# Hybrid decoder layer on one core: the heads stage traced in three runs per pair and kept in that order on TensorE, and half of the gate projection as seven products

## The chip, the cores and the metric

The kernel runs on one core of one Trainium2 chip. The metric is the device time of one execution in microseconds (us); lower is better. A run's time is the median over several executions; beside it stands one execution with a hardware profile, on which all readings of the trace rest.

## The reference

One layer over a sequence of 2048 tokens and a model width of 1024, in float32. An input projection feeds two groups of heads that read the same normalised input: 16 state-space (Mamba-2, "SSD") heads of width 64, scanned in chunks of 128 tokens, and a short gated convolution. Both outputs (together 2048 wide) go through one output projection; its result is normalised and added to the input. At the end a gate, a 1024 x 1024 projection with a sigmoid, scales a per-layer embedding that is added.

```python
h = rmsnorm(x, norm_pre)
xbc, dt_raw, z_ssd, sc_h, sc_b, sc_c, z_sc = split(h @ w_in)
xs, bm, cm = split(silu(causal_dwconv(xbc, ssd_conv_w, ssd_conv_b)))
dt = softplus(dt_raw + dt_bias)
y_ssd = ssd_chunked(xs, dt, -exp(a_log), bm, cm, d_skip)          # 16 heads of 64, chunks of 128
y_ssd = rmsnorm(y_ssd * silu(z_ssd), ssd_norm)                    # in two groups
y_sc = sc_b * causal_dwconv(sc_c * sc_h, sc_conv_w) * silu(z_sc)
mix = concatenate([y_ssd, y_sc]) @ w_out
x = x + rmsnorm(mix, norm_post)
out = x + sigmoid(x @ w_ple_gate) * (p @ w_ple_proj)
```

## The kernel before

Tokens lie along the free dimension, model columns along the 128 partitions. The 2048 tokens are two blocks of 1024 (`b`) or four groups of 512 (`tg`). Every large product is made with both operands split into two fp32r parts (the rounded value and the rest), and three of the four cross products are taken: `PASSES`, three 128x512 matmuls per 128 of the contraction. A split is a cast on ScalarE (L134 for weights, L199 for activations) and a subtraction on VectorE (L135, L200).

Weights arrive through one list, `seq`, in the order of their use. The class `Weights` keeps up to six split pieces of 128 x 4 x 128 ready (`fill`), each a load of 256 KB (L130) on SP's queue, a cast and a subtraction, and hands them out with `next`.

The program is written through a framework that tracks which instruction reads and writes which tile, sets the semaphores, and orders the instructions of each engine at compile time by its own forecast of when each is ready. The order in which the program text issues them (the order of the trace, in the words of the change) is a priority, not a command; `tc.add_manual_dep(..., NOSYNC)` fixes the order of two instructions without a semaphore. A tile pool hands a slot to a new tile when the last user of the slot's old tile is done. All loads and stores are issued on SP's queue.

The stages, one after the other, TensorE being shared between neighbours:

1. **Input projection** (to about 1032 us): products of 2x2 blocks by the seven product form (Strassen-Winograd, class `Wino`), with conv and gates behind it. Results go to DRAM: `xs_d`, `gz_d`, `cb_d`, `acs_d`, `ysc_d`, `ple_d`.
2. **Heads** (about 1032 to 1322 us). A list `steps` holds the work of the SSD heads, eight pairs of head tiles (four per block), and between the steps the generator `under()` issues `filler`: the half of the output projection that reads the short convolution (tile `os`, L838), 256 units of three matmuls, 22 of them ahead and the rest spread evenly over the steps. The work of one pair, in the names of the code and the lines of the trace:
   - `xs0`, `xs1`: load the two tiles of `xs` (L889), pool of three slots;
   - `T0`, `T1`: eight transposes each on TensorE (px, L896), then on VectorE `xd` (L903) and `xdd` (L904);
   - `load0`, `load1`: load the decays `ea` (L911, one slot, two loads of 512 KB) and the four masks `m` (L946, four slots);
   - `decays`: exp of `ea` on ScalarE (L914); `m00` to `m11`: a mask's eight exps on ScalarE (L951) and one VectorE product (L954);
   - `states`: 32 matmuls (pst, L924), then on VectorE the running state, 14 to 16 small steps (L938), and `ea` times C (L941);
   - `offsets`: 64 small matmuls from the state (py, L967);
   - `out0`, `out1`: 32 matmuls each with the masks (py, L979), then on VectorE `xs` becomes the output (L982, L983), is stored to `yz_d` (L984), squared on ScalarE (L988) and summed into `ssum` (L989).
   
   After each block `norms` adds the squares over the partitions (pn, L226) and sends the inverse norms through DRAM. `gs` makes the block's C-B products (pg, L867; pb, L879).
3. **Output projection** (to about 1512 us): `out_proj(t)` for two token groups at a time, 32 units of 24 matmuls (mo, L210); VectorE adds the part from DRAM (L1072), ScalarE squares, VectorE sums. `norm` makes the inverse norm (pn, L1084, reciprocal at L1087), `residual` scales and adds the input (L1093, L1094), `operands` splits the result.
4. **Gate** (to the end): `gate(t)`, 32 units of 24 matmuls (mg, L210); tanh on ScalarE (L1116), two VectorE steps (L1117, L1118) with the embedding `pe` (loaded at L1110), a store of 256 KB (L1119).

Steps of stages 3 and 4 are put behind numbered units (`after(unit, step)`): units 0 to 31 are the output projection, 32 to 63 the gate. Loads of two tiles at a time go through `Loads` (`L`, `L3`), three slots each.

Of the kernel before, what the change touches and what calls it, by code (L numbers as in the profile page):

```python
# [7 lines left out]
F32 = mybir.dt.float32  # L8
# [7 lines left out]
P = 128  # L16
# [38 lines left out]


@with_exitstack
def hybrid_kernel(ctx: ExitStack, tc: tile.TileContext, xT, pT, w_t, w_dt, w_o, w_g, w_p, cols_d, cst_d, outT):
# [18 lines left out]
    rs_d = [dram.tile([1, TB], F32, name=f"rs_d{b}") for b in range(NB)]  # L77
    acs_d = [dram.tile([NH, TB], F32, name=f"acs_d{b}") for b in range(NB)]

    cols = const.tile([P, NCOL], F32, name="cols")  # L80
# [56 lines left out]
    def direct(src, name, pool):  # L137
        return name, lambda sp: split_w(sp, load_w(src, name, pool), src.shape[1])
# [206 lines left out]
    for t in range(0, NG, 2):  # L345
        seq += [direct(w_o[d, :, 4 * q:4 * q + 4, :], f"o{t}_{d}_{q}", praw) for d in range(KD) for q in (0, 1)]
    for t in range(0, NG, 2):
        seq += [direct(w_g[d, :, 4 * q:4 * q + 4, :], f"g{t}_{d}_{q}", praw) for d in range(KD) for q in (0, 1)]
    W = Weights(seq)
# [3 lines left out]
    with ExitStack() as st:  # L353
# [373 lines left out]
        for b, prs, order in groups:  # L727
# [16 lines left out]
            if b + 1 < NB:  # L744
# [5 lines left out]
                if n in (6, 7, 8, 9, 10):  # L750
                    next(prep, None)

# [5 lines left out]
    class Loads:  # L758
# [5 lines left out]
        def begin(self, kind, *at):  # L764
            if (kind, *at) in self.ready:
                return
            t = self.ready[(kind, *at)] = self.pool.tile([P, 2, TG], F32, tag="ld", name="_".join(map(str, (kind, *at))))
            if kind in ("mraw", "gn"):
                b, o = divmod(at[0] * TG, TB)
            if kind == "gn":  # L770
                src = grs_d[b][:, o:o + TG].partition_broadcast(P)
            else:
                if kind == "mraw":
                    k = at[1]
                    src = yz_d[b][k:k + 2, :, o:o + TG] if k < KD else ysc_d[b][k - KD:k - KD + 2, :, o:o + TG]
                elif kind == "part":
# [37 lines left out]
    with ExitStack() as st:  # L814
# [32 lines left out]
        def heads(b):  # L847
# [34 lines left out]
            def pair(j):  # L882
# [4 lines left out]
                def loads(gr):  # L887
                    xs[gr] = t4.tile([P, TB], F32, tag="xs", name=f"xs_{b}{jts[gr]}", bufs=3)
                    nc.sync.dma_start(xs[gr], xs_d[b][jts[gr]])  # L889

                def transposes(gr):
                    jt = jts[gr]
                    px = flat(pss.tile([P, 2, TG], F32, tag="ssd", name=f"px_{b}{jt}"))
                    for c in range(NCH):
                        cs = slice(c * CH, (c + 1) * CH)
                        TE.transpose(px[:, cs], xs[gr][:, cs], ident)  # L896
                    xd[gr] = t4.tile([P, NCH, P], F32, tag="xd", name=f"xd_{b}{jt}", bufs=3)
# [113 lines left out]
        for b in range(NB):  # L1011
# [7 lines left out]
        p = pairs[0]  # L1019
        steps += [both(begins[0], p["xs0"], p["xs1"], p["load0"], p["load1"]), gs[0][0], gs[0][1], p["T0"],  # L1020
                  both(p["gz0"], p["gz1"]), p["decays"], p["T1"], no, p["m00"], no]
# [12 lines left out]
        steps += [norms[-1]]  # L1034

# [10 lines left out]


    with ExitStack() as st:
        pp = st.enter_context(tc.tile_pool(name="pp", bufs=2))
# [4 lines left out]
        def out_proj(t):  # L1054
# [25 lines left out]

        def norm(tg):

            ps = mm_bank(f"pn2_{tg}")
            TE.matmul(ps, ones_d, ssq_[tg], start=True, stop=True)  # L1084
            rs = rs_[tg] = pp.tile([P, TG], F32, tag="rs2", name=f"rs2_{tg}")
            S.activation(rs, ps, AF.Sqrt, bias=epsc[:, 0:1])
            V.reciprocal(rs, rs)  # L1087

# [11 lines left out]

        def gate(t):

            for dp in range(0, KD, 2):
                sp = []
                for tg in (t, t + 1):
                    banks = pss.tile([P, 2, TG], F32, tag="ssd", name=f"mg_{tg}_{dp}")
                    for i in range(2):
# [12 lines left out]
                        yield  # L1120


        plan = {}
# [3 lines left out]

        def second(tg, at_norm, at_res, at_ops):

            after(at_norm, lambda: norm(tg))  # L1130
# [3 lines left out]
            for n, u in enumerate(at_ops):  # L1134
                after(u, lambda d=2 * n: operands(tg, d))

        def mixes_at(tg, *units):
            m = mixes(tg, 0)
            for n, u in enumerate(units):
                after(u, *m[2 * n:2 * n + 2])  # L1140

        mixes_at(1, -1, -1, 0, 1)
        mixes_at(2, 12, 13, 14, 14)
        mixes_at(3, 15, 15, 16, 17)
        second(0, 16, (19, 20, 21, 22), (29, 29, 30, 30))
        second(1, 18, (24, 25, 26, 27), (31, 31, 32, 32))
        second(2, 32, (35, 36, 37, 38), (45, 45, 46, 46))
        second(3, 34, (40, 41, 42, 43), (47, 47, 48, 48))
        for step in plan.get(-1, ()):
            step()  # L1150
        u = 0
        for stage in (out_proj, gate):
            for t in range(0, NG, 2):
                for _ in stage(t):
                    for step in plan.get(u, ()):
                        step()
                    u += 1

# [61 lines left out]
```

## Time and profile before

| | us |
|---|---|
| median of the runs | 1691.22 (1688.46 to 1693.49) |
| the profiled execution | 1696.51, its span 1694.8 |
| TensorE (PE) busy | 1665.9, 98% of the span |
| VectorE (DVE) busy | 1248.1, 74% |
| ScalarE (ACT) busy | 780.4, 46% |
| q1, the queue of all loads and stores | 259.78 MB, 46.2% of the 16 engines' span |

"PE" is the matmuls, "PEld" the weight loads that overlap them. A group's row gives its line, engine, operation, tiles (out<-in), shapes and count, then busy time in us and mean ns of one, then the engine's idle time ahead of it and what ended that.

### The profile page before, as it was taken

The numbers are of one execution on the slowest core, as the hardware profiler recorded it, in microseconds if no ns is written. First come the engines' busy times: TensorE is split into PE (matmuls) and PEld (weight loads), VectorE is DVE, ScalarE is ACT, GpSimd is POOL, SyncE is SP. The second block draws the span as 40 slices with busy tenths as digits, with TensorE's granted clock in tenths as the row PEclk, the third lists the DMA queues.
The fourth block names the chain that finished last, engine by engine and source line by source line (L and its number), as shares of the span: only waits on it lengthen the run. The fifth ranks groups of instructions, "written<-read, shape, count | busy, mean of one in ns | idle before, by whom it ended". The sixth has DMA issues, their size and how long they took to land.

```text
span 1694.8 us, 22689 instructions
## 1 busy us (share of the span) xinstructions
PE 1665.9 (98%) x8368; PEld 1360.3 (80%) x8368; DVE 1248.1 (74%) x1837; ACT 780.4 (46%) x1402; POOL 44.8 (3%) x79
## 2 busy tenths in 40 slices
PE   9999999999999999999999999999999899999998
PEld 7888888888888888888888888787777677788886
DVE  6998778988679867778776685779587748878632
ACT  7763544434348434344444364646565324252421
POOL 0000000000000100000000000000000000000000
PEclk9999999999999999999999999999999999999999
DMA  8452322862227322121222248789787735636422
GB/s 299 155 193 81 103 93 89 265 225 106 70 69 248 108 74 100 59 88 67 106 102 83 69 146 267 233 257 293 240 298 229 244 100 168 195 103 211 148 95 87
DMA packets 121539, 261.22 MB, mean 154 GB/s; under 512 B 16970, under 2 KB 18506, under 8 KB 120404
## 3 DMA queue, kind: packets, MB, share of 16 engines
q1 hardware_dynamic: 121428, 259.78, 46.2%
q8 instruction: 65, 1.06, 0.3%
q14 instruction: 46, 0.38, 0.1%
HBM read 191.40 MB, written 68.33 MB: 153 GB/s over the span
## 4 chain that ended last, share of the span: by engine, by line
PE 88%; DMA 4%; DVE 4%; issue 2%; ACT 1%; SPq 0%; POOL 0%; DVEq 0%; POOLq 0%; ACTq 0%
PE mg L210 10%; PE mo L210 8%; PE os L838 6%; PE A_ple L210 3%; PE A_xs1X L306 1%; PE A_gc6X L306 1%; PE A_gc0X L306 1%; PE A_gc7X L306 1%; PE A_gb5X L306 1%; PE A_gb6X L306 1%; PE A_gb2X L306 1%; PE A_z1X L306 1%; PE A_z3X L306 1%; PE A_gc5X L306 1%; PE A_z2X L306 1%
## 5 line engine op out<-in xcount | busy, mean ns | idle before, releaser
L838 PE MATMUL os<-act_m,ws_os 128*128 128x512 f32 x768 | 187.8, 399 | 1.6 <-ACT po L842 0.9
L210 PE MATMUL mo<-act_m,ws_o 128*128 128x512 f32 x768 | 180.8, 396 | 4.5 <-DVE x L1072 4.5
L210 PEld LDWEIGHTS mo<-act_m,ws_o 128*128 128x128 f32 x768 | 144.1, 189 | 42.0 <-issue 6.9
L210 PE MATMUL mg<-act_x2s,ws_g 128*128 128x512 f32 x768 | 176.7, 392 | 0.7 <-ACT gth L1116 0.7
L838 PEld LDWEIGHTS os<-act_m,ws_os 128*128 128x128 f32 x768 | 142.6, 190 | 37.4 <-issue 6.6
L210 PEld LDWEIGHTS mg<-act_x2s,ws_g 128*128 128x128 f32 x768 | 143.1, 188 | 34.1 <-ACT gth L1116 4.4
L135 DVE TENSOR_TENSOR ws_A_gb<-wr_A_gb,ws_A_gb 128x512 fp32r<-128x512 f32 x96 | 65.9, 686 | 34.2 <-ACT ws_A_gb L134 34.2
L134 ACT CAST ws_A_gc<-wr_A_gc 128x512 fp32r<-128x512 f32 x96 | 59.8, 623 | 59.2 <-PE A_gc5X L306 8.3
L134 ACT CAST ws_A_gb<-wr_A_gb 128x512 fp32r<-128x512 f32 x96 | 59.6, 621 | 54.6 <-PE A_gb5Z L306 4.3
L617 DVE SCALAR_TENSOR_TENSOR xo<-ux,cols,xo 128x1024 f32<-128x1024 f32 x60 | 76.6, 1280 | 5.7 <-ACT xo L613 4.6
L951 ACT ACTIVATE m<-m,adt 128x128 f32<-128x128 f32 x256 | 77.4, 392 | 1.6 <-DMA m<-acs_d 1.5
L135 DVE TENSOR_TENSOR ws_A_gc<-wr_A_gc,ws_A_gc 128x512 fp32r<-128x512 f32 x96 | 66.0, 687 | 14.6 <-ACT ws_A_gc L134 13.2
L1117 DVE SCALAR_TENSOR_TENSOR gth<-gth,pe 128x512 f32<-128x512 f32 x32 | 22.1, 690 | 70.4 <-ACT gth L1116 70.3
L1116 ACT ACTIVATE gth<-mg 128x512 f32<-128x512 f32 x32 | 19.1, 598 | 103.7 <-PE mg L210 103.6
L954 DVE SCALAR_TENSOR_TENSOR m<-m,gsb 128x1024 f32<-128x1024 f32 x32 | 39.6, 1246 | 20.4 <-ACT m L951 18.0
L199 ACT CAST act_m<-mraw 128x512 fp32r<-128x512 f32 x64 | 38.0, 620 | 30.3 <-DVE mraw L797 15.4
L210 PE MATMUL A_ple<-act_p,ws_p 128*128 128x512 f32 x192 | 48.1, 408 | 1.9 <-ACT act_p L199 1.5
L134 ACT CAST ws_A_z<-wr_A_z 128x512 fp32r<-128x512 f32 x48 | 29.9, 623 | 42.9 <-DVE wr_A_z L183 11.7
L134 ACT CAST ws_A_xs<-wr_A_xs 128x512 fp32r<-128x512 f32 x48 | 29.9, 623 | 42.5 <-issue 11.6
L135 DVE TENSOR_TENSOR ws_A_z<-wr_A_z,ws_A_z 128x512 fp32r<-128x512 f32 x48 | 32.9, 686 | 21.2 <-ACT ws_A_z L134 21.2
L210 PEld LDWEIGHTS A_ple<-act_p,ws_p 128*128 128x128 f32 x192 | 36.6, 194 | 11.9 <-ACT act_p L199 2.5
L1072 DVE TENSOR_TENSOR x<-mo,part 128x512 f32<-128x512 f32 x32 | 21.9, 684 | 29.0 <-PE mo L210 27.6
(505 smaller groups left out, 3599.8 us busy)
## 6 DMA issues: line engine op xcount, KB each, us to landing
wr_A_gc<-in_w_t_dram SPq DMA_DIRECT2D x64, 256.0 KB, 2.6
wr_A_gb<-in_w_t_dram SPq DMA_DIRECT2D x64, 256.0 KB, 2.7
m<-acs_d SPq DMA_DIRECT2D x32, 512.0 KB, 7.2
ple_d<-A_pe SPq DMA_DIRECT2D x32, 256.0 KB, 3.5
wr_A_xs<-in_w_t_dram SPq DMA_DIRECT2D x32, 256.0 KB, 3.6
ysc_d<-vs SPq DMA_DIRECT2D x16, 512.0 KB, 2.6
wr_A_z<-in_w_t_dram SPq DMA_DIRECT2D x32, 256.0 KB, 2.9
xs_d<-xo SPq DMA_DIRECT2D x16, 512.0 KB, 3.2
```

The lines of the kernel that those rows point to most:

```text
L134: S.copy(sp[:, 0, :kn, :], raw[:, :kn, :])
L135: V.tensor_tensor(sp[:, 1, :kn, :], raw[:, :kn, :], sp[:, 0, :kn, :].bitcast(F32), ALU.subtract)
L199: S.copy(a[:, 0, :], src)
L210: TE.matmul(out, sp[:, a, (k0 + k) % 4, :], act[k0 + k][:, b, :], start=k0 + k == 0 and q == 0, stop=k0 + k == n - 1 and q == 2)
L306: TE.matmul(out, sp[:, a, k % 4, :], t[:, b, ts_], start=p in OPENS and k == 0 and q == 0, stop=k == nk - 1 and q == 2, skip_group_check=True)
L617: V.scalar_tensor_tensor(o, u[:, q:q + TB], col(w0 + q), o, ALU.mult, ALU.add)
L838: TE.matmul(ps, sp[:, a, k, :], acts_o[tg][KD + kk][:, b_, :], start=kk == 0 and n == 0, stop=kk == KD - 1 and n == 2)
L951: S.activation(m[:, c, :], m[:, c, :], AF.Exp, bias=nacs[b][:, h, c:c + 1])
L954: V.scalar_tensor_tensor(mf, mf, 1.0, s["gsb"][gr], ALU.min, ALU.mult)
L1072: V.tensor_tensor(x2[d], ps[:, i, :], pt[:, i, :], ALU.add)
L1116: S.activation(th, ps, AF.Tanh, scale=0.5)
L1117: V.scalar_tensor_tensor(th, th, 1.0, pe, ALU.add, ALU.mult)
```

## The change

It has four parts.

- **Heads.** While the heads stage is built, TensorE is wrapped (`InOrder`): each of its instructions gets an edge to the one before it, so the compiler can't move them against each other. The steps of a pair are put together: `offsets`, `out0` and `out1` in one step, `T0`, `T1` and `decays` of the next pair in one step, `states` alone. Both `xs` loads of the next pair stand with `states`; `xs` has four slots, `xd` two. The list is 117 steps long, before 127.
- **Gate of token groups 2 and 3** (`gate_seven`). The 1024 x 1024 weight is taken as 2x2 blocks of 512, the two token groups and the two halves of the contraction as the other matrix, and the seven product form computes both groups' outputs: 28 units (`GATES`, seven products with four output tiles) of 12 matmuls, in place of 16 units of 24. For it, `gate_sums` loads 16 weight tiles, makes four sums per output tile on VectorE and stores them to DRAM (`sg_d`), from where they come back through `seq`; `kept` stores x after the residual to DRAM (`x2_d`), since `operand` makes the sums of the activations in place, and it is loaded again for the last step. Products 1, 5 and 6 are copied out by ScalarE, products 2, 3 and 7 are added to a copy on VectorE before the tanh, product 4 is read from its bank. Units 32 to 47 are the old gate of groups 0 and 1 (`gate_plain`), 48 to 75 the new one.
- **Norm.** The sum over the partitions is made in columns, four one-column matmuls, root and reciprocal on 128 x 4, a diagonal of them, and one 128x512 matmul that spreads it; the two halves stand one unit apart.
- **Loads.** In the first half of the output projection the next `part` is loaded one use ahead. The residuals of groups 2 and 3 stand at units 34 to 41, before 35 to 43.

```diff
+GORDER = (1, 2, 6, 5, 3, 7, 4)
+GATES = ([(p, n) for p in (1, 2, 6) for n in range(4)]
+         + [(p, n) for h in (0, 2) for p in (5, 3) for n in (h, h + 1)]
+         + [(p, n) for p in (7, 4) for n in range(4)])
...
+    class InOrder:
...
+            def call(*a, **k):
+                inst = f(*a, **k)
+                if self.last is not None:
+                    tc.add_manual_dep(inst.ins, self.last.ins.name, NOSYNC, reason="in the order of the trace")
+                self.last = inst
+                return inst
...
+    TE = InOrder(TE)
...
-                    xs[gr] = t4.tile([P, TB], F32, tag="xs", name=f"xs_{b}{jts[gr]}", bufs=3)
+                    xs[gr] = t4.tile([P, TB], F32, tag="xs", name=f"xs_{b}{jts[gr]}", bufs=4)
...
-            steps += [both(p["states"], q["xs0"]), p["m01"], p["m10"], p["m11"], p["offsets"], p["out0"]]
-            steps += [both(q["load0"], begins[b + 1]) if fresh else q["load0"], q["T0"], both(q["decays"], q["xs1"])]
+            steps += [both(p["states"], q["xs0"], q["xs1"]), p["m01"], p["m10"], p["m11"], no,
+                      both(p["offsets"], p["out0"], p["out1"]), both(q["load0"], begins[b + 1]) if fresh else q["load0"],
+                      both(q["T0"], q["T1"], q["decays"])]
             if fresh:
-                steps += [p["out1"], q["load1"], norms[b], gs[b + 1][0], gs[b + 1][1], both(q["T1"], q["gz0"], q["gz1"]), no,
-                          q["m00"], no]
+                steps += [q["load1"], norms[b], no, gs[b + 1][0], gs[b + 1][1], both(q["gz0"], q["gz1"]), q["m00"]]
             else:
-                steps += [p["out1"], both(q["load1"], q["gz0"]), both(q["T1"], q["gz1"]), q["m00"], no]
-        steps += [norms[-1]]
+                steps += [both(q["load1"], q["gz0"]), q["gz1"], q["m00"], no, no]
+        steps += [no, no, norms[-1]]
...
+                    if t == 0:
+                        L3.begin("part", *((t + 1, dp) if tg == t else (t, dp + 2) if dp < KD - 2 else (t + 2, 0)))
...
+            def sums():
+                ssq = ssq_[tg]
+                ps = mm_bank(f"pn2_{tg}")
+                for c in range(TG // P):
+                    TE.matmul(ps[:, c:c + 1], ssq[:, c * P:(c + 1) * P], ones_d[:, 0:1], start=True, stop=True)
...
+            def spread():
+                ps = mm_bank(f"prs2_{tg}")
+                TE.matmul(ps, ones_d, ssq_[tg], start=True, stop=True)
+                rs = rs_[tg] = pp.tile([P, TG], F32, tag="rs2", name=f"rs2_{tg}")
+                S.mul(rs, ps, float(D))
...
+        def kept(tg, d):
+            for i in range(2):
+                nc.sync.dma_start(x2_d[tg][d + i], x2s_[tg][d + i])
+
+        def gate_sums(n):
+
+            w = []
+            for i, h in ((0, 0), (0, 1), (1, 0), (1, 1)):
+                w.append(tmp(f"sg_{n}_{i}{h}"))
+                nc.sync.dma_start(w[-1].rearrange("p (k c) -> p k c", c=P), w_g[n + 4 * i, :, 4 * h:4 * h + 4, :])
+            yield
+            a, b, c, d = w
+            V.tensor_tensor(d, c, d, ALU.add)
+            V.tensor_tensor(c, c, a, ALU.subtract)
+            V.tensor_tensor(a, a, d, ALU.subtract)
+            V.tensor_tensor(b, b, a, ALU.add)
+            for i, v in enumerate((d, a, c, b)):
+                nc.sync.dma_start(sg_d[n][i], v.rearrange("p (k c) -> p k c", c=P))
+            yield
...
+            if p == 6:
+                src = tmp(f"t2_{k}")
+                V.tensor_tensor(b11, b12, b11, ALU.subtract)
+                V.tensor_tensor(src, b11, b22, ALU.subtract)
+                V.tensor_tensor(b21, b21, src, ALU.add)
+            elif p == 7:
+                src = b12
+                V.tensor_tensor(b12, b12, b22, ALU.subtract)
+            else:
+                src = {1: b11, 2: b21, 5: b11, 3: b22, 4: b21}[p]
+            ops_.setdefault(p, []).append(split_act(src, f"x2s_{p}{k}", FIRST[g % 4]))
...
+            for m, (p, n) in enumerate(GATES):
+                if m + 2 < len(GATES) and GATES[m + 2][1] % 2 == 0 and at(*GATES[m + 2]):
+                    L.begin("pe", *at(*GATES[m + 2]))
+                    L3.begin("x2", *at(*GATES[m + 2]))
...
+                out, sp = bank[BANK[p], n], W.next()
+                for k in range(4):
+                    for q, (a, b) in enumerate(PASSES):
+                        TE.matmul(out, sp[:, a, k, :], ops_[p][k][:, b, :], start=p in OPENS and k == 0 and q == 0,
+                                  stop=k == 3 and q == 2, skip_group_check=True)
+                if p in (1, 5, 6):
+                    keep[p, n] = tmp(f"kp_{t}_{p}{n}")
+                    S.copy(keep[p, n], out)
+                else:
+                    finish(*at(p, n), out, keep.get(({2: 1, 3: 6, 7: 5, 4: 0}[p], n)))
...
+        second(2, 32, (34, 35, 36, 37))
+        second(3, 34, (38, 39, 40, 41))
+        for n in range(4):
+            sums = gate_sums(n)
+            for u in (36, 38):
+                after(u + 2 * n, lambda sums=sums: next(sums))
+        operands_at(0, 45, 46)
+        operands_at(1, 46, 47)
+        operands_at(2, 48, 49, 50, 51)
+        operands_at(3, 52, 53)
+        operands_at(4, 54, 55)
+        operands_at(5, 57, 59)
+        operands_at(6, 61, 63)
```

More of the change, by code (lines that the diff above doesn't have):

```diff
@@ L78, in hybrid_kernel @@
     acs_d = [dram.tile([NH, TB], F32, name=f"acs_d{b}") for b in range(NB)]
+    sg_d = [dram.tile([4, P, 4, P], F32, name=f"sg_d{n}") for n in range(KD // 2)]
+    x2_d = {g: dram.tile([KD, P, TG], F32, name=f"x2_d{g}") for g in range(NG // 2, NG)}
     cols = const.tile([P, NCOL], F32, name="cols")
@@ L751, in hybrid_kernel, with __init__, __getattr__ @@
                     next(prep, None)
+    class InOrder:
+        def __init__(self, engine):
+            self.engine, self.last = engine, None
+        def __getattr__(self, name):
+            f = getattr(self.engine, name)
+            def call(*a, **k):
[4 more added lines that the diff above has]
+                return inst
+            return call
+    TE = InOrder(TE)
     pss = ctx.enter_context(tc.tile_pool(name="pss", bufs=3, space=PSUM))
@@ L1019, in hybrid_kernel @@
         p = pairs[0]
-        steps += [both(begins[0], p["xs0"], p["xs1"], p["load0"], p["load1"]), gs[0][0], gs[0][1], p["T0"],
-                  both(p["gz0"], p["gz1"]), p["decays"], p["T1"], no, p["m00"], no]
+        steps += [both(begins[0], p["xs0"], p["xs1"], p["load0"], p["load1"]), gs[0][0], gs[0][1], both(p["T0"], p["T1"]),
+                  both(p["gz0"], p["gz1"]), p["decays"], p["m00"], no]
         for n, p in enumerate(pairs):
@@ L1045, in hybrid_kernel @@
             pass
+    TE = nc.tensor
     with ExitStack() as st:
@@ L1079, in out_proj, with norm @@
                         yield
[L1081 to L1087, printed above, removed]
+        def norm(tg, unit):
+            def sums():
[3 more added lines that the diff above has]
+                    TE.matmul(ps[:, c:c + 1], ssq[:, c * P:(c + 1) * P], ones_d[:, 0:1], start=True, stop=True)
+                q = const.tile([P, TG // P], F32, tag="rq2", name=f"rq2_{tg}")
+                S.activation(q, ps[:, 0:TG // P], AF.Sqrt, bias=epsc[:, 0:1])
+                V.reciprocal(q, q)
+                V.tensor_tensor(ssq.rearrange("p (c t) -> p c t", t=P), ident.unsqueeze(1).to_broadcast([P, TG // P, P]),
+                                q.unsqueeze(2).to_broadcast([P, TG // P, P]), ALU.mult)
+            def spread():
[3 more added lines that the diff above has]
+                S.mul(rs, ps, float(D))
+            after(unit, sums)
+            after(unit + 1, spread)
         def residual(tg, d):
@@ L1120, in gate, with tmp @@
                         yield
+        def tmp(name):
+            return pp.tile([P, TG], F32, tag="x2", name=name, bufs=NG * KD)
+        def kept(tg, d):
[15 more added lines that the diff above has]
+            yield
@@ L1126, in after, with second @@
             plan.setdefault(unit, []).extend(steps)
-        def second(tg, at_norm, at_res, at_ops):
-            after(at_norm, lambda: norm(tg))
+        def second(tg, at_norm, at_res):
+            norm(tg, at_norm)
             for n, u in enumerate(at_res):
@@ L1133, in second, with operands_at @@
                 after(u, lambda d=2 * n: residual(tg, d))
-            for n, u in enumerate(at_ops):
-                after(u, lambda d=2 * n: operands(tg, d))
+                if tg in x2_d:
+                    after(u + 1, lambda d=2 * n: kept(tg, d))
+        def operands_at(g, *units):
+            for k in range(4):
+                after(units[k * len(units) // 4], lambda k=k: operand(g, k))
         def mixes_at(tg, *units):
@@ L1140, in mixes_at @@
                 after(u, *m[2 * n:2 * n + 2])
+        L3.begin("part", 0, 0)
         mixes_at(1, -1, -1, 0, 1)
@@ L1144, in hybrid_kernel @@
         mixes_at(3, 15, 15, 16, 17)
[L1145 to L1148, printed above, removed]
+        second(0, 16, (19, 20, 21, 22))
+        second(1, 18, (24, 25, 26, 27))
+        for tg, units in ((0, (29, 29, 30, 30)), (1, (31, 31, 32, 32))):
+            for n, u in enumerate(units):
+                after(u, lambda tg=tg, d=2 * n: operands(tg, d))
+        second(2, 32, (34, 35, 36, 37))
[11 more added lines that the diff above has]
+        operands_at(6, 61, 63)
         for step in plan.get(-1, ()):
@@ L1151, in hybrid_kernel @@
         u = 0
[L1152 to L1157, printed above, removed]
+        for stage, t in ((out_proj, 0), (out_proj, 2), (gate_plain, 0), (gate_seven, 2)):
+            for _ in stage(t):
+                for step in plan.get(u, ()):
+                    step()
+                u += 1
 _OUTS = [((KD, P, T), 'float32')]
```

50 lines of the change are left out of this document (44 added, 6 removed).

## The prediction

> **What bounds the kernel now.** I read the page first, then the busy times by stage, then TensorE's waits, then the order of its runs in the heads stage.
>
> ```profile
> span 1694.8 us, 22689 instructions
> PE 1665.9 (98%) x8368; PEld 1360.3 (80%) x8368; DVE 1248.1 (74%) x1837; ACT 780.4 (46%) x1402; POOL 44.8 (3%) x79
> ```
>
> TensorE is busy 98% of the span, so time is won by fewer or denser TensorE instructions, or by taking away the waits in the other 2%. The stages (start:end, length, busy time of each engine, granted clock, DMA share, GB/s):
>
> ```profile
> 1260.00:1265.00 5.00, 4.18 (x23) 3.04 (x22) 2.98 (x3) 4.55 (x15) 0.00 (x0) 1.00 1.02 407
> ...
> 1032.00:1322.00 290.00, 275.88 (x2266) 221.26 (x2268) 210.75 (x313) 164.36 (x380) 6.99 (x12) 0.99 0.81 260
> 1322.00:1512.00 190.00, 184.51 (x784) 146.02 (x781) 129.07 (x191) 65.88 (x107) 0.00 (x0) 0.98 0.49 161
> 1512.00:1600.00 88.00, 88.00 (x383) 71.14 (x382) 66.33 (x97) 34.45 (x54) 0.00 (x0) 1.00 0.51 169
> 1600.00:1689.40 89.40, 88.65 (x388) 71.75 (x386) 31.88 (x49) 17.91 (x33) 0.00 (x0) 1.00 0.30 105
> 1689.40:1694.80 5.40, 0.00 (x0) 0.00 (x0) 1.38 (x2) 0.57 (x1) 0.00 (x0) 0.71 0.13 49
> ```
>
> Second row: the heads stage, the only one where TensorE idles (14 us) while VectorE (210.75 of 290) and the DMA engines (0.81) are both well loaded. Then the output projection, the two halves of the gate (TensorE full), and a tail of 5.4 us. What TensorE waits for after 1030 us:
>
> ```profile
> PE pn L226 <- DVE ssum L989: 6.4, 3, 3.6
> PE px L896 <- DMA xs<-xs_d: 6.1, 3, 2.7
> PE mo L210 <- DVE x L1072: 4.5, 4, 2.2
> PE os L838 <- ACT po L842: 0.9, 1, 0.9
> ...
> PE mg L210 <- ACT gth L1116: 0.7, 1, 0.7
> ```
>
> And one pair of heads on TensorE (start, length, instructions, idle before them), with three later places:
>
> ```profile
> 1208.48 0.44 PE L967 MATMUL py<-ea,sprev 64*64 64x128 f32 x4
> 1208.85 0.77 PE L896 MATMUL px<-cst,xs 128*128 128x128 f32 x5
> 1209.55 1.96 PE L967 MATMUL py<-ea,sprev 64*64 64x128 f32 x60
> 1211.44 1.97 PE L979 MATMUL py<-m,xd 128*64 128x128 f32 x32
> 1213.34 0.55 PE L896 MATMUL px<-cst,xs 128*128 128x128 f32 x3
> 1213.81 1.97 PE L979 MATMUL py<-m,xd 128*64 128x128 f32 x32
> 1215.71 11.63 PE L838 MATMUL os<-act_m,ws_os 128*128 128x512 f32 x50
> 1229.87 1.07 PE L896 MATMUL px<-cst,xs 128*128 128x128 f32 x8 [2.53 <-DMA xs<-xs_d]
> ...
> 1231.48 4.08 PE L838 MATMUL os<-act_m,ws_os 128*128 128x512 f32 x11
> ...
> 1295.58 1.84 PE L896 MATMUL px<-cst,xs 128*128 128x128 f32 x8 [2.73 <-DMA xs<-xs_d]
> ```
> ```profile
> 1326.94 29.70 PE L210 MATMUL mo<-act_m,ws_o 128*128 128x512 f32 x122
> ```
>
> The compiler's order cuts one pair's work into pieces (4 and 60, 5 and 3), and a wait over 2.5 us is followed by slow matmuls.
>
> **The change, part by part.** A 128x512 matmul in steady flow:
>
> ```profile
> 1517.59 10.92 PE mg L210 x48
> ```
>
> 0.2275 us each. *Seven products.* Token groups 2 and 3 took 384 matmuls (8 outputs, 2 groups, 8 k, 3 passes); 28 products of 4 k and 3 passes are 336. 48 fewer: **-10.9 us**, if nothing else holds TensorE.
>
> *What the seven products cost VectorE.* Times per instruction, and the spacing of back to back ones:
>
> ```profile
> L135 DVE TENSOR_TENSOR ws_g<-wr_g,ws_g 128x512 fp32r<-128x512 f32 x32 | 21.9, 685 | 10.3 <-ACT ws_g L134 10.3
> ```
> ```profile
> 1356.54 0.68 DVE L135 TENSOR_TENSOR ws_o<-wr_o,ws_o 128x512 fp32r<-128x512 f32 x1
> 1357.14 0.68 DVE L1072 TENSOR_TENSOR x<-mo,part 128x512 f32<-128x512 f32 x1
> ```
>
> So 0.60 to 0.69 us each. In the 28 units (76.4 us of TensorE) VectorE has about 23 weight splits (five are made ahead), 36 operand steps and 44 finishing steps: 103, or 62 to 71 us. It fits on the whole, not everywhere: units 48 to 51 hold 20 of them (12.0 to 13.8 against 10.9 us) and 52 to 55 hold 24 (14.4 to 16.6), so VectorE falls 4.6 to 8.6 us behind. What hides it: weights are issued five pieces, 13.6 us, ahead. If that cover went, TensorE would wait for the weight split next. Bounds 0 to +6, taken **+2**. The third product of a bank waits for ScalarE's copy of the first, eight units earlier: nothing. The tail has the same tanh, two VectorE steps and one store: nothing.
>
> *DMA in the first half of the gate.* Into units 35 to 47 (13 x 5.46 = 71 us) the change brings 16 stores of x2, 16 loads and 16 stores for the weight sums, beside 39 loads and stores that were there and 12 pieces of xres: 99 pieces of 0.262 MB, 26 MB. At 407 GB/s (first row of the stages) that is 64 us; at the heads stage's 260/0.81 = 321 GB/s it is 81. On SP's queue a store waits for the residual's VectorE step, and a load of the sums for a buffer that the gate's last step frees; behind them stand the loads of pe, whose two buffers give them 11 us, and of weights, with a longer lead. Bounds 0 to +10, taken **+3**, nearer the 407 end, since these are plain 2 KB rows like that window's, where the heads also load broadcasts. The Trainium skill, "DMA: Bandwidth & Descriptors", section "Where 436 GB/s comes from", says that transfers between HBM and SBUF are bound at about 358 GB/s per core; by it, an estimate, these 26 MB take 73 us and the term would be nearer +6. This trace's 407 over 5 us disagrees, for bursts at least.
>
> *Heads in program order, three runs per pair.* The work in the seven rows from 1208.48 to 1215.71 is 64 L967 (60 in 1.89 us), 64 L979 (32 in 1.90) and 8 px (about 0.9): 2.0 + 3.8 + 0.9 = 6.7, and it took 7.23. Merged runs give back 0.5 per pair, 8 pairs: -4.1 us. *xs loaded a pair ahead, with a fourth buffer*: the loads no longer follow the store of the pair before, which takes the px waits, -6.1. *Norms later*: last outputs come ten steps before the final norm instead of five, first block four steps instead of two: the pn waits, -6.4; os, -0.9. *Slow clock behind those waits*: os x11 should take 10 x 0.2275 + 0.39 = 2.7, so 1.4; px x8 1.84 against 1.07, 0.8; mo x122 29.7 against 27.9, 1.8: -4.0. Together **-21.5**. The Trainium skill, "TensorE: Matmul & The Clock Gate", Part 1, puts the halving behind an idle window of about 3.4 us; the rows here show it after 2.53 us. By that rule the px waits would carry no such term, 2.2 less of a gain.
>
> *What the new order adds there.* Both outputs of a pair now stand together and need all four masks; the decays stand one step behind their load. The path from one pair's L967 to the next pair's second output:
>
> ```profile
> L951 ACT ACTIVATE m<-m,adt 128x128 f32<-128x128 f32 x256 | 77.4, 392 | 1.6 <-DMA m<-acs_d 1.5
> ...
> L954 DVE SCALAR_TENSOR_TENSOR m<-m,gsb 128x1024 f32<-128x1024 f32 x32 | 39.6, 1246 | 20.4 <-ACT m L951 18.0
> ...
> L938 DVE SCALAR_TENSOR_TENSOR sprev<-sprev,ea,pst 128x64 f32<-128x64 f32 x112 | 22.2, 274 | 4.9 <-issue 4.0 <-PE pst L924 0.9
> ...
> L941 DVE SCALAR_TENSOR_TENSOR ea<-ct,ea 128x1024 f32<-128x1024 f32 x16 | 18.8, 1218 | 0.0
> ...
> L914 ACT ACTIVATE ea<-ea 128x2048 f32<-128x2048 f32 x8 | 15.3, 1918 | 8.7 <-DMA ea<-acs_d 8.7
> ```
> ```profile
> ea<-acs_d SPq DMA_DIRECT2D x16, 512.0 KB, 11.2
> ```
>
> Load 11.2, exp 1.9, four masks of 77.4/32 = 2.4, the last VectorE mask 1.2: 24.0 us. TensorE's period: 234 filler units over 116 steps are 26 in a pair's 13 steps (26 x 3 x 0.2275 = 17.8), the heads take 9.4 (L967 2.0, L979 3.8, px 1.7, pst 1.9 at L979's rate), and five changes at the 0.5/4 us of the seven rows 0.6: 27.8. To the next second output it is 2 more, 29.8. Room 5.8 us, so the masks are in time. But at the stage's new length (about 277) the same work loads VectorE 76% and the DMA engines 85%, so some waits come back. Next late would be the offsets: behind pst stand 14 state steps (22.2/8 = 2.8) and two ea steps (2.4), 5.2 us under five steps of filler, 6.9. Then the masks, when ScalarE is held by a load of ea: with that cover gone, the copy of an os bank is late too, and TensorE waits within two banks. Bounds: 0, and all 21.5 and more (the rivals); taken 0.9 per pair, **+7**. On SP, xs is moved ahead of the stores of yz and waits for no buffer there; the loads of ea and m stand behind L967 and L979 as they did, and one behind another. Nothing moves on POOL.
>
> *Norm in columns, part prefetched.* Four one-column matmuls per group are added; the first input has the same form:
>
> ```profile
> 39.86 0.95 PE L404 MATMUL A_ssq<-ones_d,ssq 128*128 128x1 f32 x8
> ```
> ```profile
> L1087 DVE RECIPROCAL rs<-rs 128x512 f32<-128x512 f32 x4 | 13.4, 3344 | 0.6 <-ACT rs L1086 0.6
> ```
>
> At most 4 x 0.95 = +3.8 on TensorE. VectorE loses 3.3 and gains some 0.8 per group, which shortens the mo waits behind it (4.5): -3.1 taken, and the mg wait of 0.7 goes: **0** in sum, bounds -2 to +4.
>
> Sum: -10.9 + 2 + 3 - 21.5 + 7 + 0 = -20.4. The profiled execution took 1696.51 (span 1694.8 and 1.7 around it), 5.3 above the median of 1691.22; I set the difference on the median: 1670.8, forecast **1670**.
>
> **Rivals.**
> *The waits return in the heads stage.* If DMA at 85% lands ea and xs late as before, or TensorE's order hardly changes, the waits stay and only the runs count: -4 - 5.9 = **1681**; without those too, **1685**. For: ea takes 11.2 us and the stage is at 0.81 already. Against: xs gets a period of room, and px was the DMA wait.
> *The gate's saving is eaten.* +10 and +6 instead of +3 and +2: the gate loses 5.1, heads -14.5: **1682**. For: 99 pieces in 71 us. Against: the two deep loads have leads over 10 us.
> *Slower: the masks bind every pair.* In program order TensorE can't do filler past an output whose mask is late. Once the load of ea and m takes over 11.2 + 5.8 = 17 us, each further us is a wait in all eight pairs, and from 2.5 us on it brings 1.4 of slow clock. It decides (over +0.3%, what can be told from no change here) at -20.4 - 7 + 8x > 5, x about 4: a landing near 20 us. At 5 us a pair: -27.4 + 40, **1704**. For: the merged outputs free all buffers at once, so all loads queue together. Against: at the first row's 407 GB/s the 4.2 MB that queue there (ea, four masks, two stores of yz) clear in 10.3 us.
> *All covers hold*: no new waits, -32.4: **1659**; 1657 with the norm's lower bound, and the range goes to 1650 for pieces and waits under 0.5 us elsewhere in the stage that no term counts.
>
> **How the numbers follow.** Forecast 0.57 (own range 1660 to 1679); waits return 0.17, half of it within 0.3%; gate eaten 0.11; slower 0.08; all covers hold 0.07. Faster by over 0.3% (under 1686): 0.57 + 0.11 + 0.07 + 0.09 = 0.84; same 0.08; slower 0.08. The range 1650 to 1687 leaves out little more than the slow case.
>
> **What would show it.** Right: mg has 720 matmuls, the heads stage some 277 us, no wait of px for xs, ssum waits under 2 us, changes between os and heads in three places per pair, gate halves of 87 to 91 and 76 to 80 us. Wrong: py or pst waiting for m, ea or xdd for over 2 us per pair; mg waiting for weights or gth while the DMA share is near 1; VectorE or DMA filling the heads stage.

## The result and the profile after

The changed kernel takes 1673.45 us (median, 1671.42 to 1678.72), the kernel before 1691.76 on the same chip: 18.3 us less, a ratio of 0.9894 with a 95% interval of 0.9873 to 0.9915. The forecast was 1670, range 1650 to 1687. The profiled execution took 1674.55 us, 1.1 above its median, where the one of before (1696.51) stood 4.8 above 1691.76; so the spans differ by 22.0 us, 3.7 more than the medians, and the readings below add up to 22.

The page of the changed kernel:

```profile
span 1672.8 us, 22881 instructions
PE 1647.1 (98%) x8352; PEld 1350.9 (81%) x8352; DVE 1278.3 (76%) x1909; ACT 800.0 (48%) x1442; POOL 45.6 (3%) x79
```

TensorE is 18.8 us shorter and stays at 98%; VectorE has 30 us more to do. Its stages (columns as before):

```profile
1032.00:1306.50 274.50, 265.67 (x2272) 219.86 (x2273) 211.76 (x314) 162.35 (x379) 7.82 (x12) 0.99 0.83 272
1306.50:1498.00 191.50, 187.02 (x810) 149.10 (x809) 126.40 (x197) 69.40 (x115) 0.00 (x0) 1.00 0.54 174
1498.00:1584.50 86.50, 83.22 (x368) 66.90 (x367) 59.33 (x97) 28.21 (x44) 0.00 (x0) 1.00 0.82 273
1584.50:1667.40 82.90, 82.17 (x355) 65.28 (x353) 70.52 (x112) 41.20 (x74) 0.00 (x0) 1.00 0.67 222
```

To compare kernels I cut the span at TensorE's own work, each cut at the start of an instruction: heads from the first os matmul to the last os or pn, output projection to the last mo, gate to the end of the last matmul. Mo or mg matmuls that stand ahead of a cut are moved over it at 0.2275 us each. "Changes" are the places in the heads where one TensorE instruction is of another kind than the one before it.

| kernel | heads | changes | output projection | gate |
|---|---|---|---|---|
| before | 292.7 | 116 | 185.6 | 178.4 |
| changed | 274.0 | 68 | 186.9 | 174.1 |
| heads part alone | 277.4 | 68 | 185.9 | 178.4 |
| gate, norm and loads alone | 291.3 | 116 | 183.7 | 175.6 |
| changed, no fixed order | 269.8 | 71 | 186.3 | 176.2 |
| fixed order, old list and slots | 298.0 | 108 | 185.6 | 172.9 |
| no fixed order, new list, 3 slots of xs | 289.4 | 102 | 187.3 | 175.3 |
| no fixed order, old list, xs early, 4 slots | 284.4 | 123 | 183.5 | 176.4 |
| no fixed order, sums early | 269.2 | 71 | 190.8 | 169.8 |
| the same, sums spaced | 271.4 | 71 | 191.5 | 169.8 |
| fixed order, sums early and spaced | 276.8 | 68 | 192.5 | 169.9 |
| changed, old norm | 277.4 | 68 | 186.0 | 173.3 |

So the 22 us are 18.7 from the heads and 4.3 from the gate, less 1.3 lost in the output projection.

Each row is one execution, and that sets how finely the column of the heads can be read. The four kernels with the new list, four slots and fixed order run the same instructions of this stage in the same order on TensorE, VectorE and ScalarE, and read 274.0, 276.8, 277.4 and 277.4; the three with the same list and slots and no fixed order also agree in order (but for one VectorE instruction at the edge of the stage) and read 269.2, 269.8 and 271.4. So 2 to 3.5 us there separate executions of one order, and the changed kernel's 274.0 is the lowest of its four.

What TensorE waits for after 1000 us in the changed kernel:

```profile
PE mg L220 <- ACT ws_g L144: 3.3, 1, 3.3
PE pst L779 <- DVE xdd L943: 3.1, 3, 2.4
PE py L779 <- DVE m L993: 2.7, 1, 2.7
PE mo L220 <- DVE x L1115: 1.8, 2, 1.5
PE pn L779 <- DVE ssum L1028: 1.6, 1, 1.6
PE mo L220 <- ACT act_m L209: 1.5, 2, 1.0
PE mo L220 <- DVE act_m L210: 1.2, 3, 0.8
```

The wait of px for xs (6.1) is gone, pn fell from 6.4 to 1.6, and new ones came: the states for `xdd`, an output for a mask, the first mo matmuls for their operands, the gate for a weight. One pair of heads on TensorE:

```profile
1090.56 1.97 PE L779 MATMUL pst<-xdd,btok 128*64 128x128 f32 x32
1092.45 7.09 PE L779 MATMUL os<-act_m,ws_os 128*128 128x512 f32 x30
1099.48 1.98 PE L779 MATMUL py<-ea,sprev 64*64 64x128 f32 x64
1101.38 3.71 PE L779 MATMUL py<-m,xd 128*64 128x128 f32 x64
1105.03 3.02 PE L779 MATMUL os<-act_m,ws_os 128*128 128x512 f32 x12
1107.89 1.91 PE L779 MATMUL px<-cst,xs 128*128 128x128 f32 x16
1109.55 8.43 PE L779 MATMUL os<-act_m,ws_os 128*128 128x512 f32 x36
```

Three whole runs, and 27.4 us from one pst to the next (1090.56 to 1117.92 us) where the forecast reckoned 27.8 without waits.

### The profile page after: what moved, and what is told of

Same layout as the page of the kernel before. It is cut to its first block, busy times and chain, and to the rows that moved or that the text cites. A ratio compares the mean times of both kernels' runs of the same rounds, so it can differ in the third digit from the quotient of the medians.

```text
span 1672.8 us, 22881 instructions
## 1 busy us (share of the span) xinstructions
PE 1647.1 (98%) x8352; PEld 1350.9 (81%) x8352; DVE 1278.3 (76%) x1909; ACT 800.0 (48%) x1442; POOL 45.6 (3%) x79
## 4 chain that ended last, share of the span: by engine, by line
PE 87%; DMA 5%; DVE 4%; ACT 2%; issue 1%; SPq 1%; DVEq 0%; ACTq 0%
PE mo L220 9%; PE os L779 6%; PE mg L220 3%; PE mg_X L1259 3%; PE A_ple L220 3%; PE mg_Y L1259 2%; DMA mraw<-yz_d 2%; PE A_xs1X L316 1%; PE A_gc0X L316 1%; PE A_gc6X L316 1%; PE A_gb7X L316 1%; PE A_gb5X L316 1%; PE A_gc7X L316 1%; PE A_z3X L316 1%; PE A_xs3X L316 1%; PE A_gb6X L316 1%
## 5 line engine op out<-in xcount | busy, mean ns | idle before, releaser
L779 PE MATMUL os<-act_m,ws_os 128*128 128x512 f32 x768 | 184.3, 396 | 1.0 <-ACT A_z L714 0.7
L220 PE MATMUL mg<-act_x2s,ws_g 128*128 128x512 f32 x384 | 90.4, 394 | 3.3 <-ACT ws_g L144 3.3
L220 PEld LDWEIGHTS mg<-act_x2s,ws_g 128*128 128x128 f32 x384 | 71.3, 188 | 20.8 <-ACT ws_g L144 3.7
L145 DVE TENSOR_TENSOR ws_A_gc<-wr_A_gc,ws_A_gc 128x512 fp32r<-128x512 f32 x96 | 66.1, 688 | 14.4 <-ACT ws_A_gc L144 13.1
L209 ACT CAST act_m<-mraw 128x512 fp32r<-128x512 f32 x64 | 38.1, 621 | 31.7 <-DVE mraw L836 18.7
L210 DVE TENSOR_TENSOR act_m<-mraw,act_m 128x512 fp32r<-128x512 f32 x64 | 41.8, 685 | 6.7 <-ACT act_m L209 6.4
L1259 PE MATMUL mg_X<-act_x2s,ws_g 128*128 128x512 f32 x192 | 45.6, 393 | 0.7 <-ACT gth L1230 0.7
```

The source lines that it names most:

```text
L145: V.tensor_tensor(sp[:, 1, :kn, :], raw[:, :kn, :], sp[:, 0, :kn, :].bitcast(F32), ALU.subtract)
L209: S.copy(a[:, 0, :], src)
L210: V.tensor_tensor(a[:, 1, :], src, a[:, 0, :].bitcast(F32), ALU.subtract)
L220: TE.matmul(out, sp[:, a, (k0 + k) % 4, :], act[k0 + k][:, b, :], start=k0 + k == 0 and q == 0, stop=k0 + k == n - 1 and q == 2)
L779: inst = f(*a, **k)
L1259: TE.matmul(out, sp[:, a, k, :], ops_[p][k][:, b, :], start=p in OPENS and k == 0 and q == 0, stop=k == 3 and q == 2, skip_group_check=True)
```

## The experiments

The theory behind the prediction: the heads lose cut runs and the waits for xs and the norm, the gate loses 48 matmuls and pays a part back in transfers, and the parts add up. The main rivals: the fixed order itself is the gain, or the early xs alone, or the parts help each other.

**The heads part alone**, put into the kernel before.

```diff
+    TE = InOrder(TE)
...
-                    xs[gr] = ... bufs=3)
+                    xs[gr] = ... bufs=4)
...
-                    xd[gr] = ... name=f"xd_{b}{jt}", bufs=3)
+                    xd[gr] = ... name=f"xd_{b}{jt}")
...
-        steps += ...   # the list of before
+        steps += ...   # the new list
...
+    TE = nc.tensor
```

> The kernel before with the heads part alone: step list, fixed order, four slots for xs. Theory A (the parts add up): the heads stage is 274 to 276 us from its first os to the first mo matmul, some 19 us under before, the rest as before, so 1673 to 1677 us. Rival B (much of the 18 us needs the other parts, since the output projection begins with more waits when the heads end sooner): the heads stage is 275 us, but the output projection is 4 us or more longer, 1679 to 1683 us.

1679.54 us, ratio 0.9929 (0.9913 to 0.9946). The time lies in B's range, but B's reason falls: the output projection is not longer (185.9). The heads are 277.4, not 274 to 276, so A's time was 3 us too low; the same order of instructions read 274.0 in the changed kernel.

**The gate, norm and loads alone**: the changed kernel with the heads stage of before.

```diff
-    TE = InOrder(TE)
...
-                    xs[gr] = ... bufs=4)
+                    xs[gr] = ... bufs=3)
...
-                    xd[gr] = ... name=f"xd_{b}{jt}")
+                    xd[gr] = ... name=f"xd_{b}{jt}", bufs=3)
...
-        steps += ...   # the new list
+        steps += ...   # the list of before
```

> The changed kernel with the heads stage of before: seven products, norm in columns, part prefetched. Theory A: gate 4 to 5 us shorter, output projection 0 to 2 us longer by the norm's one-column matmuls, so 1687 to 1690 us. Rival B (the stage is as full as the transfers allow, and only in the changed kernel do they come at a good time): gate saving under 2 us, 1690 to 1693 us.

1688.96 us, ratio 0.9982 (0.9967 to 0.9996), in theory A's range, by another split than A's: gate 2.8 us and output projection 1.9 us shorter, the second because mo waits less for VectorE (4.5 us before):

```profile
PE mo L220 <- DVE x L1092: 1.7, 2, 0.9
```

The two ratios multiply to 0.9911; the whole change has 0.9894, whose interval (0.9873 to 0.9915) holds it. The parts add up, as far as these intervals can tell.

**Without the fixed order.**

```diff
-    TE = InOrder(TE)
```

> The changed kernel without the edges that fix TensorE's order in the heads stage; the step list and the four slots of xs stay. Theory A (the fixed order is what keeps the runs whole): the compiler cuts runs again, over 90 changes of kind in the stage instead of 58, and the stage is 4 to 9 us longer, 1677 to 1682 us. Rival B (the grouping in the list is enough): 58 to 70 changes, within 2 us of the changed kernel. Rival C (the fixed order costs waits that the compiler's order avoids): shorter than the changed kernel by 3 us or more.

1670.66 us, ratio 0.9875 (0.9858 to 0.9892). Theory A falls. The compiler keeps the runs whole without edges, from the new list with the early xs, 71 changes against 68:

```profile
1092.13 1.97 PE L941 MATMUL pst<-xdd,btok 128*64 128x128 f32 x32
1094.03 7.09 PE L855 MATMUL os<-act_m,ws_os 128*128 128x512 f32 x30
1101.05 1.98 PE L984 MATMUL py<-ea,sprev 64*64 64x128 f32 x64
1102.95 3.71 PE L996 MATMUL py<-m,xd 128*64 128x128 f32 x64
1106.60 3.02 PE L855 MATMUL os<-act_m,ws_os 128*128 128x512 f32 x12
```

Row for row the lengths of the changed kernel. Yet its heads stage is 4.2 us shorter, as in rival C. The times alone don't tell the two kernels apart (2.8 us, and the intervals of the ratios overlap); a pair of runs on one chip, further down, does. TensorE's order in the stage is nearly the same (2265 of 2272 matmuls stand in the same sequence); VectorE's is not. In the changed kernel it stands still ahead of one pair's states:

```profile
1234.83 0.75 DVE L836 SCALAR_TENSOR_TENSOR mraw<-mraw,cols,gn 128x512 f32<-128x512 f32 x1 [4.47 <-DMA mraw<-yz_d]
...
1245.35 1.22 DVE L943 TENSOR_TENSOR xdd<-xd,dst 128x1024 f32<-128x1024 f32 x1
```

A step for the output projection, not needed before 1306 us, waits 4.5 us for its load at the head of VectorE's queue; `xdd` ends at 1246.6, and pst, begun at 1243.85, waits for it 2.4 us, with slow matmuls behind it. Without the edges `xdd` is done at 1241.6 and pst runs through at 1243.72. The edges left TensorE's order nearly as it was and changed the order that the compiler gave VectorE. All four kernels with the new list and edges have this stall (4.5 to 6.8 us ahead of that step) and the same wait of 2.4 us of pst behind it. In the three without edges the step comes behind that pair's states (1254 to 1258 us, waiting 0.3 to 3.3 us), and those states wait for nothing. That this one step makes the whole difference was read from these rows and not tried.

**Fixed order with the old list and slots**, in the changed kernel.

```diff
-                    xs[gr] = ... bufs=4)
+                    xs[gr] = ... bufs=3)
...
-                    xd[gr] = ... name=f"xd_{b}{jt}")
+                    xd[gr] = ... name=f"xd_{b}{jt}", bufs=3)
...
-        steps += ...   # the new list
+        steps += ...   # the list of before
```

> The changed kernel with the step list and slots of before in the heads stage, in fixed order. Theory A: fewer cut runs than before, but the second xs load still follows a store of yz, so TensorE waits for px some 6 us as before; stage 282 to 288 us, 1680 to 1686 us. Rival B (fixed order alone brings the gain): 1672 to 1676 us. Rival C (fixed order with this list makes TensorE wait behind each late mask or transfer): over 290 us in the stage, 1689 us or more.

1697.53 us, ratio 1.0038 (1.0023 to 1.0052), slower than before, though it holds the shorter gate. Rival C:

```profile
PE px L779 <- DMA xs<-xs_d: 14.4, 6, 6.3
PE pn L779 <- DVE ssum L1028: 3.4, 2, 3.3
```

The late xs costs 14.4 us where the compiler's own order before the change, which had up to 50 os matmuls in a row ahead of px, had 6.1. Here the fixed order is only as good as the list.

**New list with three slots of xs**, no fixed order.

```diff
-    TE = InOrder(TE)
...
-                    xs[gr] = ... bufs=4)
+                    xs[gr] = ... bufs=3)
...
-                    xd[gr] = ... name=f"xd_{b}{jt}")
+                    xd[gr] = ... name=f"xd_{b}{jt}", bufs=3)
```

> No fixed order. The new step list, but three slots for xs: the second xs load of the next pair, although issued early, has to wait for the store of yz. The run without the order (four slots) had 71 changes of kind, no px wait, 269.8 us in the heads stage. Theory A (the early xs is worth its px waits with what follows them): px waits of 6 to 14 us return, stage 278 to 286 us, 1678 to 1686 us. Rival B (the list alone makes the gain, since the next pair's transposes now come later behind the stores): px waits under 3 us, stage under 273 us, 1669 to 1674 us.

1690.34 us, ratio 0.9990 (0.9975 to 1.0005). Px waits for xs again, as theory A says:

```profile
PE px L913 <- DMA xs<-xs_d: 7.9, 5, 2.7
```

But the loss is larger than A's range (stage 289.4 against 278 to 286): the runs are cut again, 102 changes. So with this list the slots don't only take a wait away, they also keep the runs whole; that the compiler's forecast sees the late data and splits the runs for it is the likely reason, not shown. The slots of xd go back to three with this edit and were not tried apart.

**Old list with xs early and four slots**, no fixed order. Against the list of before:

```diff
-            steps += [both(p["states"], q["xs0"]), p["m01"], ...
+            steps += [both(p["states"], q["xs0"], q["xs1"]), p["m01"], ...
-            steps += [..., q["T0"], both(q["decays"], q["xs1"])]
+            steps += [..., q["T0"], q["decays"]]
```

> No fixed order. The step list of before, but both xs loads beside the states and four slots. Theory A (list and early xs are separate gains): px waits vanish, but 105 to 120 changes of kind stay and the last norm waits as before; stage 280 to 286 us, 1678 to 1684 us. Rival B (early xs is the whole gain): stage under 273 us, 1669 to 1674 us. Rival C (nothing without the list): over 288 us, 1686 us or more.

1681.8 us, ratio 0.9941 (0.9927 to 0.9955). Theory A in stage and time: px does not wait for xs, 123 changes stay. The last norm, against A, hardly waits (pn 0.3). What waits instead, and the step ahead of the longest of these waits on VectorE:

```profile
PE pst L941 <- DVE xdd L921: 8.1, 3, 6.6
```
```profile
1243.36 0.75 DVE L814 SCALAR_TENSOR_TENSOR mraw<-mraw,cols,gn 128x512 f32<-128x512 f32 x1 [8.47 <-DMA mraw<-yz_d]
```

That is the stall of the output projection's step again, here without any edge.

So without the order: neither 291.3 (the stage in the kernel with gate, norm and loads alone), list alone 289.4, early xs alone 284.4, both 269.8. Alone they give 1.9 and 6.9, together 21.5. The 1.9 is no more than what two executions differ by, so the list without early data gives little or nothing. The 6.9 holds the stall: without that wait of 6.6 us and the 1.7 of slow pst matmuls behind it (3.68 us where 1.96 is usual), early xs alone would give some 15, an estimate. So most of the 21.5 may be the early xs; how much the two need each other stays open.

**The sums of the gate's weights early**, no fixed order.

```diff
-            for u in (36, 38):
+            for u in (4, 6):
```

> The changed kernel without the fixed order, and the weight sums made at units 4 to 12 of the output projection in place of 36 to 44. Theory A (TensorE's wait for a gate weight is the queue of transfers in the gate's first half): that wait of 3.3 to 3.7 us and the slow matmuls behind it vanish, DMA share there falls from 0.82 to about 0.7, gate 3 to 4 us shorter than in the run without the order, output projection unchanged; 1666 to 1668 us. Rival B (the wait is that of one load stuck on SP behind a store that waits for VectorE): it stays or moves, 1669 to 1672 us. Rival C (the sums now hold up the start of the output projection, where loads of mraw are late already): output projection 3 us longer or more, 1671 us or more.

1667.64 us, ratio 0.9861 (0.9844 to 0.9878), the lowest time of all and ahead of the changed kernel, but not to be told from the run without the order (0.9858 to 0.9892). Theory A for the gate: the wait for ws_g is gone, and the gate is 6.4 us shorter than without the move (169.8 against 176.2), more than A's 3 to 4. Here 90 us of the gate's first half in the run without the order, then with the sums moved:

```profile
1490.00:1580.00 90.00, 86.28 (x375) 69.59 (x374) 62.03 (x102) 30.72 (x48) 0.00 (x0) 0.98 0.79 265
```
```profile
1490.00:1580.00 90.00, 90.00 (x400) 73.07 (x400) 63.66 (x103) 33.48 (x53) 0.00 (x0) 1.00 0.68 225
```

In 90 us TensorE does 25 matmuls more, and the DMA share falls from 0.79 to 0.68. But rival C holds too: the output projection grew by 4.5 us. VectorE there:

```profile
DVE sg L1173 <- DMA sg<-in_w_g_dram: 16.1, 4, 5.5
```

**The same with the sums two units further from their loads.**

```diff
-            for u in (4, 6):
+            for u in (4, 8):
```

> No fixed order, weight sums in the output projection as in the run before, but four units between a tile's loads and its sums (units 4 to 10 and 8 to 14) in place of two. Theory A (there VectorE stood before sums whose load had not landed, and the output's next step behind it): VectorE's wait for sg falls from 16 us to under 4, the four waits of mo of 0.9, 2.2, 0.4 and 0.1 us go, output projection 187 us, gate still 170, 1663 to 1666 us. Rival B (the sums' own time on VectorE is what the output projection lacks): output projection 189 us or more, 1667 us or more.

1669.28 us, ratio 0.9868 (0.9850 to 0.9885). Theory A falls:

```profile
DVE sg L1173 <- DMA sg<-in_w_g_dram: 16.8, 4, 5.3
```

The wait is unchanged, and the traces say why: from the first mo to the last, TensorE, VectorE and ScalarE run the same instructions in the same order in both kernels. The first sums begin 9.1 us after the issue of their loads there (1330.86 to 1339.92 us) and 8.9 us here (1333.43 to 1342.34). The compiler put the step where it had been, so this is the run before once more; what a longer distance would bring, and whether B holds, was not seen.

**The fixed order once more**, on the same chip as the run before and with the same sums.

```diff
+    TE = InOrder(TE)
```

> The same places for the weight sums, with the fixed order of the changed kernel in the heads stage. Theory A (the fixed order itself costs some 4 us of waits of pst for xdd): 3 to 5 us above the run without it on the same chip, heads stage 274 us against 270. Rival B (the 3 us between the changed kernel and the run without the order were that day's chip): within 1.5 us of it.

1675.88 us, ratio 0.9910 (0.9896 to 0.9924), 6.6 us above the run without the edges, and the intervals do not meet. Heads 276.8 against 271.4, and again

```profile
PE pst L779 <- DVE xdd L943: 4.1, 3, 2.4
```

against 1.1 us without them. The stalled step stands ahead of that wait here too:

```profile
1236.04 0.75 DVE L836 SCALAR_TENSOR_TENSOR mraw<-mraw,cols,gn 128x512 f32<-128x512 f32 x1 [6.36 <-DMA mraw<-yz_d]
```

In the output projection the engines' order is the same in both kernels (192.5 against 191.5), and the gate is equal (169.9 and 169.8). Theory A, with more than its 3 to 5 us.

**The old norm** in the changed kernel.

```diff
-            norm(tg, at_norm)
+            after(at_norm, lambda: norm(tg))   # norm as before the change
```

> The changed kernel with the norm of before: one 128x512 matmul, root and reciprocal over 512 columns. Theory A (the two forms cancel: 0.8 us of one-column matmuls per group against 2.5 us of VectorE): output projection and gate within 1.5 us in sum, 1672 to 1675 us. Rival B (the reciprocal's 3.3 us bring back the waits of the output projection for VectorE): 3 us or more longer, 1676 us or more. Rival C (VectorE has room since the heads end sooner): the 3.2 us of one-column matmuls are saved, 1669 to 1671 us.

1673.88 us, ratio 0.9900 (0.9879 to 0.9921): theory A in time, no difference that can be told. Output projection and gate together are 359.3 against 361.0 us, 1.7 shorter where A had at most 1.5.

## Why the prediction was right

It holds as a whole (-20.4 forecast, -18.3 measured), and most terms by their sign; the named cause of the largest one does not. That the total came so close is in part luck. By stages of the profile the heads gained 18.7 where the sum gives 12.7, the gate 4.3 where it gives 5.9, and the output projection lost 1.3 where a gain of 1.8 was forecast; and 3.7 of the 22 us come from the profiled execution of before, which stands that much further above its median. By medians the heads part alone gave 13.1 us (1692.68 to 1679.54).

*Seven products, -10.9, and the transfers, +3.* Mg and its kin are 720 matmuls, 336 of them the new ones. The gate was to change by -10.9 + 2 + 3 = -5.9 and changed by -4.3; two norms stand in it, which cost 1.2 more in columns than before (2.5 against 1.3). Cut at the last matmul of groups 0 and 1, its halves were 89.4 and 89.0 and are 95.1 and 79.0: the second as the forecast's signs say (76 to 80), the first above them (87 to 91). The second half gave 10.0 of the 10.9. The 5.7 more in the first are the norms, a wait of 3.3 and 1.2 of small pauses. That wait, for the transfers, came in the half that the forecast named, and it is one of its signs of being wrong (mg waiting for weights with the DMA engines nearly full):

```profile
1519.14 54.29 PE L220 MATMUL mg<-act_x2s,ws_g 128*128 128x512 f32 x235
1576.69 6.50 PE L220 MATMUL mg<-act_x2s,ws_g 128*128 128x512 f32 x26 [3.26 <-ACT ws_g L144]
```

with ScalarE behind loads and stores that queue (first the store of an older result, whose buffer the tanh needs, then the weight):

```profile
1566.16 0.60 ACT L1174 ACTIVATE gth<-mg 128x512 f32<-128x512 f32 x1 [8.13 <-DMA out_dram<-gth]
...
1576.02 1.92 ACT L144 CAST ws_g<-wr_g 128x512 fp32r<-128x512 f32 x3 [3.29 <-DMA wr_g<-in_w_g_dram]
```

The DMA engines are busy 0.91 at 305 GB/s in 1520 to 1600 us:

```profile
1520.00:1600.00 80.00, 76.72 (x333) 61.55 (x332) 61.47 (x100) 26.88 (x47) 0.00 (x0) 1.00 0.91 305
```

That is 335 GB/s at full share, nearer the 321 than the 407 of the forecast's two rates. It is not beyond the 358 that the Trainium skill's "DMA: Bandwidth & Descriptors" names (section "Where 436 GB/s comes from"): over this long stretch of loads and stores the trace agrees with it, over the 5 us with 407 it did not. At 335 the 26 MB take 78 us where 71 were counted, 7 too much; that the wait was only 3.3 may be the lead that the weights have, which was not tried. Moving the sums away shows the price of making them there (loads, stores and VectorE steps together), 6.4 us without the fixed order; the forecast's +3 was small. The +2 for VectorE was not found: in the seven product half the only wait left is mg's 0.7 for gth, as before.

*Heads, -21.5 + 7.* The stage gained 18.7 us where the sum gives 12.7 up to the first mo (the 1.8 of slow matmuls beyond it left out). The px waits went as said, pn gave back 4.8 of 6.4. The mis-sized term is *merged runs, -4.1*: I counted the seven rows of one pair, without the pst matmuls in 2 and 30. Over all changes, from the start of the instruction ahead of a change to the start of the one behind it, less waits and that kind's usual spacing (os 0.227 us, px 0.109, pst 0.059, py 0.030 from the state and 0.058 with the masks), they cost 14.4 us before (116) and 6.1 after (68): -8.3. All waits of the stage (over 0.15 us each) went from 14.6 to 8.5 us, -6.1 where the forecast's terms add to -6.4; what is left, slow matmuls and small pauses, fell by 4.2 where 2.2 was forecast. The new waits, +7, are 3.1 (pst for xdd) + 2.7 (py for a mask) + 0.8 (py for ea) = 6.6 in the trace. That this size is right is in part luck: the forecast put it down to a fuller VectorE and fuller DMA engines, and more than a third of it (2.6) is `xdd` behind the one stalled step.

*The cause that was named.* "Heads in program order" was taken for what keeps the runs whole. The runs without the edges show that the list and the early xs do it. The edges cost 6.6 us in the pair of runs on one chip; over all seven kernels of this list and these slots the heads are 276.4 us with them and 270.1 without, on the mean. The rival "slower: the masks bind every pair" did not come: one wait of 2.7 us for a mask in eight pairs. Nor did the waits return: with the edges taken away, list and slots together give 21.5 us.

*Norm and part prefetch, 0.* For the norm the run with the old one in the changed kernel bears it out; the prefetch of `part` was not tried alone. The mo waits were shortened with the heads of before (4.5 to 1.7 us). In the changed kernel they moved: 4.5 us before (for x), 4.5 after, of which 2.7 are for operands of the second unit. The heads end 20 us sooner there, and VectorE stands before a load of yz that the operands need:

```profile
1311.63 2.08 DVE L836 SCALAR_TENSOR_TENSOR mraw<-mraw,cols,gn 128x512 f32<-128x512 f32 x3 [3.68 <-DMA mraw<-yz_d]
```

*The slow clock.* The forecast put 4.0 us behind waits from 2.5 us on; after the change one 2.37 us wait is followed by slow matmuls, and those of 2.70 us (py) and 3.26 us (mg, granted clock 1.00 in that stage) are not. So my 2.5 us does not tell which wait is followed. The Trainium skill's idle window of about 3.4 us ("TensorE: Matmul & The Clock Gate", Part 1) is free-running by the same page; the wait of 2.37 us is shorter than it, and that figure does not tell either.

## What to carry to other kernels

When a compiler cuts runs into pieces, look first for the data that come late: with xs early, the same list gave whole runs without any fixed order, and a fixed order on the old list was slower than before. An edge on one engine also changed the compiler's order on another, so compare the queues of all engines, and look for steps of a later stage that stand there waiting for a load. After an edit, see that the order of the instructions changed at all: one edit here moved nothing. Price a saving in matmuls together with the transfers it brings. Moving those to a stage with less traffic took 6.4 us from the gate and cost 4.5 in the output projection, where VectorE then waited for them.

## What the runs showed of the hardware

A change of matmul shape on TensorE (the 128*128, 128*64 or 64*64 that a row names first) costs time in these traces: from os in 128*128 to pst in 128*64 or py in 64*64 0.09 us beyond the usual spacing, back to os 0.14, from py in 64*64 to py in 128*64 0.17; 14.4 us over the 116 changes of before. In the changed kernel px between os matmuls, 128*128 both, costs nothing. I had not expected so much for so small a thing. TensorE's granted clock can fall behind a wait of 2.37 us, seen in the 30 pst matmuls behind it, 2.85 us where 1.96 is usual, and in the granted clock, 0.64 in that stretch:

```profile
1246.62 2.85 PE L779 MATMUL pst<-xdd,btok 128*64 128x128 f32 x30 [2.37 <-DVE xdd L943]
```
```profile
1246.60:1250.00 3.40, 3.38 (x32) 2.96 (x33) 3.11 (x5) 3.40 (x13) 0.00 (x0) 0.64 1.04 421
```
